# The low halves of split weights at the other end of SBUF, and a feed-forward block in four rounds

## The chip, the cores and the metric

One program runs on one core of a Trainium2 chip. The metric is the device time of one execution in microseconds (us). The kernel before was timed three times: 2065.13, 2066.44 and 2067.92 us, median 2066.44 us. One execution was profiled.

## The reference

One layer of a streaming encoder for 384 frames: 256 frames of a new stream and 16 frames each of eight running streams. All is float32.

```
h = rmsnorm(x) ; p = h @ w_in                      (2048 x 9224)
A = swish(layernorm(causal_dwconv31(GLU(p)))) @ conv_pw_out
B = fox_attention(q, k, v, logf) @ w_att_out       (past keys and values from a cache)
x = x + (sigmoid(gate_a) * A + sigmoid(gate_b) * B) @ w_out
up = rmsnorm(x) @ w_up                             (2048 x 11264; half g, half u)
x = x + (silu(causal_dwconv3(g)) * u) @ w_down     (5632 x 2048)
```

It returns the two groups' outputs, the new keys, values, forget logits, and the conv states.

## The kernel before, in words

**Split matmuls.** Each float32 operand is split into a high half `hi` (rounded to the type float32r) and a low half `lo`, the rest. One product takes three TensorE matmuls into one PSUM accumulator: high by high, high by low, low by high (lines 241 to 243 in a "B" job, where the activations are the stationary operand and the weights stream as the moving one; lines 236 to 238 in an "A" job, the other way round). `gemm` (line 219) runs a list of jobs: a B job makes a 384 x 512 piece of the output in three accumulators (one for each 128 frames), in steps of k, 128 rows of the weight each: 3 accumulators x 3 matmuls for a k.

**Weights.** They come in units of two k: SyncE's queue loads `raw` (128 x 2 x 512, line 137), ScalarE rounds it to `hi` (line 145), VectorE subtracts and gets `lo` (line 146). `raw`, `hi` and `lo` have three buffers each, and `ahead(3)` keeps three units split ahead of TensorE. The list `plan` fixes the units' order.

**Order.** TensorE's instructions stand in the order in which the code is written (`manual_schedule`). The other engines' orders are made by a scheduler with priorities: splits and evacuations of PSUM are pulled forward (`SPLIT_AHEAD`, `EVAC_AHEAD`). Each engine then works strictly through its own list.

**Feed-forward block.** Up-projection group g (of 11) is two B jobs of 16 k: the gate half and the u half of 512 columns. ScalarE evacuates each job into `tok` (line 936). VectorE turns it round with 16 block transposes (line 943), then for g the three-tap conv (964, 966), for u the product with the gate (987) and the low half of the activation (990). The result `act{g}` is a tile of the pool `acts`. In the 11th k after a g job a small transpose on TensorE (973) brings the new conv state out. `down_jobs` multiplies the `act` tiles of some groups by `w_down`: four B jobs, one for each 512 output columns, with four k for each group; VectorE adds every accumulator to the residual `y` (line 1006). `FFN_PLAN` says which groups are gathered into a down round: groups 0 to 3 after up group 4, groups 4 to 7 after up group 8, groups 8 to 10 at the end.

**PSUM.** Five accumulators of 128 x 512 (`acc`) go round in turn; a B job takes three. So the third accumulator of a job is the first one of the job before, which must have been evacuated.

**SBUF.** Pools are stacked from both ends of a partition. From the bottom: `hi` (2 to 14 KB), the pool `acts` with five slots G0 to G4 of 12 KB (14 to 76 KB; first `hT`, the normed input, then `mix`, then `act`), then `xg` (76 to 125 KB, the input of the up-projection) or, earlier, the attention's tiles. From the top: constants, `lo` (212 to 224 KB), `raw` (200 to 212 KB), then the attention output, the conv pool, or, later, `y` and the feed-forward pool. `ut`, the conv branch's 12 KB tile, uses slot G4.

Of the kernel before, what the change touches and what calls it, by code (L numbers as in the profile page):

```python
# [8 lines left out]
F32 = mybir.dt.float32  # L9
F32R = mybir.dt.float32r  # L10
# [5 lines left out]
P = 128  # L16
DM = 2048
NT = 384
# [22 lines left out]
def hybrid_step(  # L41
# [11 lines left out]
    def pool(name, side="left", bufs=1, space=None):  # L53
        kw = dict(name=name, bufs=bufs, reuse_waits="tile")
        if space is not None:
            kw["space"] = space
        else:
            kw["side"] = side
        cm = tc.tile_pool(**kw)
        p = cm.__enter__()  # L60
        return p, lambda: cm.__exit__(None, None, None)

    cp, close_cp = pool("consts", side="right")
    rp, close_rp = pool("raw_lo", side="right")
    wp, close_wp = pool("hi")
    gp, close_gp = pool("acts")
    acc, close_acc = pool("acc", bufs=5, space=PSUM)
    misc, close_misc = pool("misc", bufs=3, space=PSUM)
# [70 lines left out]
        return raw, o  # L139

    def split_tiles():
        return [p.tile([P, 2, 512], F32R, tag=tag, bufs=3, name=tag) for p, tag in ((wp, "hi"), (rp, "lo"))]

    def split_rows(hi, lo, raw, o, k):
        nc.scalar.copy(hi[:, k, :o], raw[:, k, :o])  # L145
# [2 lines left out]
    def split(raw, o):  # L148
        hi, lo = split_tiles()
        split_rows(hi, lo, raw, o, slice(0, 2))  # L150
        return hi, lo
# [3 lines left out]
    def planned(w, k0, cols, nk, *more):  # L155
        for k in range(k0, k0 + nk, 2):
            for cl in (cols,) + more:
                plan.append([w[0, k * P:(k + 2) * P, c:c + n].rearrange("(k p) n -> p k n", p=P) for c, n in cl])
# [8 lines left out]
    GA_COLS = [[(O_GA + 512 * g, 512)] for g in range(4)]  # L167
    GB_COLS = [[(O_GB + 512 * g, 512)] for g in range(4)]
    N_COLS = [[(512 * g, 512)] for g in range(4)]
    FFN_PLAN = [("up", g) for g in range(5)] + [("down", (0, 1, 2, 3))]  # L170
    FFN_PLAN += [("up", g) for g in range(5, 9)] + [("down", (4, 5, 6, 7))]
    FFN_PLAN += [("up", g) for g in range(9, 11)] + [("down", (8, 9, 10))]

    planned(w_in, 0, V_COLS[0], 16, V_COLS[1])
# [2 lines left out]
    for w, nk in ((w_att_out, 8), (conv_pw_out, 8), (w_out, 16)):  # L177
        for cols in N_COLS:
            planned(w, 0, cols, nk)
    for what, g in FFN_PLAN:  # L180
        if what == "up":
# [36 lines left out]
    def gemm(jobs, sides=()):  # L218
        for js in jobs:
            js = js if isinstance(js, tuple) else (js,)  # L220
            for j in js:
                nb = 4 if j["kind"] == "A" else NTT
                j["ps"] = [(misc_tile if j is not js[0] and i == 2 else acc_tile)() for i in range(nb)]
            for j, k in [(j, k + i) for k in range(0, js[0]["nk"], 2) for j in js for i in range(2)]:
                nb, n, nk, ps = len(j["ps"]), j["n"], j["nk"], j["ps"]
                kk = k % 2
                if kk == 0:
                    ahead(3)
                    hi, lo = ready.pop(0)
                ah, al = j["act"](k)  # L230
                st, sp = k == 0, k == nk - 1
                for m in range(nb):
                    s = slice(m * P, (m + 1) * P)
                    if j["kind"] == "A":
                        o = ps[m][:, :NT]
                        mm(o, hi[:, kk, s], ah, start=st, stop=False)  # L236
                        mm(o, hi[:, kk, s], al, start=False, stop=False)  # L237
                        mm(o, lo[:, kk, s], ah, start=False, stop=sp)  # L238
                    else:
                        o = ps[m][:, :n]  # L240
                        mm(o, ah[:, s], hi[:, kk, :n], start=st, stop=False)  # L241
                        mm(o, ah[:, s], lo[:, kk, :n], start=False, stop=False)  # L242
                        mm(o, al[:, s], hi[:, kk, :n], start=False, stop=sp)  # L243
                if sp:
                    with tc.high_priority(offset=EVAC_AHEAD):
                        for m in range(nb):
                            j["evac"](m, ps[m])
                    if "done" in j:
                        j["done"]()
                tick(sides)  # L250
# [5 lines left out]
    def job(kind, nk, act, evac, n=512, done=None):  # L256
        d = dict(kind=kind, nk=nk, act=act, evac=evac, n=n)
        if done is not None:
            d["done"] = done
        return d  # L260
# [20 lines left out]
    with tc.manual_schedule(engines={ENG.SP, ENG.Activation, ENG.DVE}):  # L281
        nc.vector.memset(junk[:, 0:1], 0.0)
        nc.scalar.dma_start(gm_row[:], norm_mix_g[0].rearrange("(c p) -> c p", p=P))
        nc.scalar.activation(junk[:, 1:2], junk[:, 0:1], AF.Identity)
        load_x(0, 1)
        first = stream_tile()
        fetch_row(first, plan[0], 0)
        load_x(1, 1)
        fetch_row(first, plan.pop(0), 1)
        second = fetch(plan.pop(0))  # L290
        load_x(2, 2)
        warm = misc_tile()

        def warm_up(n):
            for _ in range(n):
                mm(warm[:, :P], ident[:], ident[:], start=True, stop=True)

        warm_up(WARM)
        pv = misc_tile()
        tr(pv[:, :16], gm_row[:], ident[:16, :16])  # L300
        nc.vector.tensor_copy(gm[:], pv[:, :16])
        hi, lo = split_tiles()
        split_rows(hi, lo, first, V_COLS[0][0][1], slice(0, 1))
        x_chunk(0)
        warm_up(FILL)
        split_rows(hi, lo, first, V_COLS[0][0][1], slice(1, 2))
        x_chunk(1)
        ready.append((hi, lo))
        ready.append(split(*second))
# [17 lines left out]
    p_cv, close_cv = pool("conv", side="right")  # L327
# [324 lines left out]
            yield  # L652


    ut = gp.tile([P, 8, NT], F32, tag="G4", name="ut")

    sgb = [None, None]

# [88 lines left out]
    for h in range(H):  # L747
        hi, lo = aHL[h // 4][:, 0, h % 4, :], aHL[h // 4][:, 1, h % 4, :]
# [180 lines left out]
    acts = {}  # L929

    def tok_rows():
        return p_f.tile([P, NTT, 512], F32, tag="tok", bufs=1, name="tok")

    def up_evac(rows):
        def ev(t, ps):
            nc.scalar.activation(rows[:, t, :], ps[:], AF.Identity, scale=rs2[:, t:t + 1])
        return ev
# [44 lines left out]
    def up_u_done(g, rows, sg):  # L982
        def done():
            uT = p_f.tile([P, 4, NT], F32, tag="uT", bufs=1, name="uT")
            blocks(rows, lambda a, js: uT[js].rearrange("p m (t a i) -> p m t a i", t=NTT, a=4)[:, :, :, a])
            for m in range(4):
                tt(uT[:, m], uT[:, m], sg[m][:], op=ALU.mult)
                hi, lo = acts[g][:, 0, m, :], acts[g][:, 1, m, :]
                nc.scalar.copy(hi, uT[:, m])
                tt(lo, uT[:, m], f(hi), op=ALU.subtract)  # L990
        return done

    def up_jobs(g):
        sg = [p_f.tile([P, NT], F32, tag="sg", bufs=6, name="sg") for _ in range(4)]
        acts[g] = gp.tile([P, 2, 4, NT], F32R, tag=f"G{g % 5}", name=f"act{g}")
        gr, ur = tok_rows(), tok_rows()
        return [job("B", 16, xa, up_evac(gr), done=up_g_done(g, gr, sg)),
                job("B", 16, xa, up_evac(ur), done=up_u_done(g, ur, sg))]

    def down_jobs(gs, last):  # L1000
        tiles = [acts[g] for g in gs]

        def evac(n):
            def ev(t, ps):
                ys = y[:, t, n * 512:(n + 1) * 512]
                tt(ys, ps[:], ys, op=ALU.add)
                if last:
                    dst = [y_prompt[0, 0:P], y_prompt[0, P:2 * P], y_sample.rearrange("b t d -> (b t) d")][t]
                    nc.sync.dma_start(dst[:, n * 512:(n + 1) * 512], ys)
            return ev  # L1010

        return [job("B", 4 * len(gs), grouped(tiles), evac(n)) for n in range(4)]

    for what, g in FFN_PLAN:
        gemm(up_jobs(g) if what == "up" else down_jobs(g, g[-1] == 10))
# [45 lines left out]
```

## Time and profile before

| | |
|---|---|
| median of three runs | 2066.44 us |
| profiled execution, its own time | 2065.19 us |
| its span in the profile | 2063.4 us |
| TensorE (PE) busy | 2051.4 us, 9606 matmuls |
| VectorE (DVE) busy | 1189.5 us |
| ScalarE (ACT) busy | 755.7 us |
| DMA | 276.00 MB, mean 134 GB/s |
| granted TensorE clock | 0.999 of full |

A row of a group reads: line, engine, operation, output <- inputs, shape, count, then busy time in us and mean ns of one, then the engine's idle time just before these instructions and what ended it. Matmuls overlap in a pipeline, and their ends are modelled: one of 512 columns is shown with about 0.39 us, yet the next begins about 0.23 us after it. The steady pace is thus read from starts or from counts in a window, not from durations. PEld is the load of the stationary operand. Idle time in front of TensorE is the only idle time that costs something here.

### The profile page before, as it was taken

The numbers are of one execution on the slowest core, as the hardware profiler recorded it, in microseconds if no ns is written. First come the engines' busy times: TensorE is split into PE (matmuls) and PEld (weight loads), VectorE is DVE, ScalarE is ACT, GpSimd is POOL, SyncE is SP. The second block draws the span as 40 slices with busy tenths as digits, with TensorE's granted clock in tenths as the row PEclk, the third lists the DMA queues.
The fourth block names the chain that finished last, engine by engine and source line by source line (L and its number), as shares of the span: only waits on it lengthen the run. The fifth ranks groups of instructions, "written<-read, shape, count | busy, mean of one in ns | idle before, by whom it ended". The sixth has DMA issues, their size and how long they took to land.

```text
span 2063.4 us, 24707 instructions
## 1 busy us (share of the span) xinstructions
PE 2051.4 (99%) x9606; PEld 1700.8 (82%) x9606; DVE 1189.5 (58%) x1722; ACT 755.7 (37%) x1099; POOL 97.3 (5%) x214
## 2 busy tenths in 40 slices
PE   9999999999999999999999999999999999999999
PEld 8878999988888888887888888888888888888887
DVE  4434477788762645344676776533676764337662
ACT  5434455533332523333333333322333332223321
POOL 1000011100000000000000001000100100001000
PEclk9999999999999999999999999999999999999999
DMA  6555455344444353333444444344444433344443
GB/s 180 158 165 162 138 160 163 114 140 128 133 128 123 123 184 121 125 124 116 123 123 132 125 123 132 124 132 124 125 122 133 127 127 126 130 125 124 133 147 108
DMA packets 175742, 276.00 MB, mean 134 GB/s; under 512 B 11998, under 2 KB 63217, under 8 KB 175617
## 3 DMA queue, kind: packets, MB, share of 16 engines
q1 hardware_dynamic: 175305, 273.84, 43.8%
q8 instruction: 75, 1.23, 0.2%
q0 software_dynamic: 288, 0.57, 0.2%
q14 instruction: 42, 0.34, 0.1%
q10 hardware_dynamic: 32, 0.01, 0.0%
HBM read 266.98 MB, written 7.86 MB: 133 GB/s over the span
## 4 chain that ended last, share of the span: by engine, by line
PE 97%; DVE 1%; ACT 1%; DMA 0%; issue 0%; SPq 0%; ACTq 0%
PE acc L243 29%; PE acc L241 29%; PE acc L242 29%; PE acc L236 2%; PE acc L238 2%; PE acc L237 2%; DVE lo L146 0%; DMA raw<-in_w_in_dram 0%; ACT hi L145 0%; DVE uT L943 0%; PE misc L559 0%; PE misc L836 0%; PE misc L883 0%; PE misc L625 0%; PE misc L592 0%
## 5 line engine op out<-in xcount | busy, mean ns | idle before, releaser
L146 DVE TENSOR_TENSOR lo<-raw,hi 128x1024 fp32r<-128x1024 f32 (+2 forms) x481 | 580.4, 1207 | 775.1 <-ACT hi L145 768.6
L145 ACT CAST hi<-raw 128x1024 fp32r<-128x1024 f32 (+2 forms) x481 | 496.3, 1032 | 1116.9 <-PE acc L243 989.8
L241 PE MATMUL acc<-hi,xg 128*128 128x512 f32 x1056 | 418.3, 396 | 0.0
L243 PE MATMUL acc<-hi,xg 128*128 128x512 f32 x1056 | 416.0, 394 | 0.0
L242 PE MATMUL acc<-lo,xg 128*128 128x512 f32 x1056 | 414.8, 393 | 0.0
L241 PE MATMUL acc<-hi,hT 128*128 128x512 f32 (+1 forms) x704 | 271.3, 385 | 2.9 <-ACT vt L413 1.7
L243 PE MATMUL acc<-hi,hT 128*128 128x512 f32 (+1 forms) x704 | 269.3, 383 | 1.8 <-DVE hT L277 1.8
L242 PE MATMUL acc<-lo,hT 128*128 128x512 f32 (+1 forms) x704 | 268.2, 381 | 0.0
L243 PEld LDWEIGHTS acc<-hi,xg 128*128 128x128 f32 x1056 | 198.3, 188 | 47.0
L241 PEld LDWEIGHTS acc<-hi,xg 128*128 128x128 f32 x1056 | 198.2, 188 | 46.5
L242 PEld LDWEIGHTS acc<-lo,xg 128*128 128x128 f32 x1056 | 198.5, 188 | 45.4
L243 PE MATMUL acc<-hi,act 128*128 128x512 f32 x528 | 208.5, 395 | 0.2 <-DVE act L990 0.2
L241 PE MATMUL acc<-hi,act 128*128 128x512 f32 x528 | 207.8, 394 | 0.0
L242 PE MATMUL acc<-lo,act 128*128 128x512 f32 x528 | 207.0, 392 | 0.0
L243 PEld LDWEIGHTS acc<-hi,hT 128*128 128x128 f32 x704 | 132.9, 189 | 29.4 <-DVE hT L277 3.8
L241 PEld LDWEIGHTS acc<-hi,hT 128*128 128x128 f32 x704 | 133.1, 189 | 28.5 <-ACT vt L413 2.3
L711 DVE SCALAR_TENSOR_TENSOR ut<-ext,cw,ut 128x384 f32<-128x384 f32 x240 | 151.8, 632 | 6.1
L242 PEld LDWEIGHTS acc<-lo,hT 128*128 128x128 f32 x704 | 133.2, 189 | 24.8
L243 PEld LDWEIGHTS acc<-hi,act 128*128 128x128 f32 x528 | 99.1, 188 | 23.5 <-DVE act L990 0.6
L242 PEld LDWEIGHTS acc<-lo,act 128*128 128x128 f32 x528 | 99.2, 188 | 23.4
L241 PEld LDWEIGHTS acc<-hi,act 128*128 128x128 f32 x528 | 99.1, 188 | 22.3
L943 DVE STREAM_TRANSPOSE uT<-tok 32x384 f32<-32x384 f32 x176 | 100.2, 570 | 2.6
(290 smaller groups left out, 2076.4 us busy)
## 6 DMA issues: line engine op xcount, KB each, us to landing
raw<-in_w_up_dram SPq DMA_DIRECT2D x176, 512.0 KB, 3.6
raw<-in_w_in_dram SPq DMA_DIRECT2D x96, 512.0 KB, 3.6
raw<-in_w_down_dram SPq DMA_DIRECT2D x88, 512.0 KB, 3.6
raw<-in_w_in_dram SPq DMA_DIRECT2D x64, 256.0 KB, 3.0
raw<-in_w_out_dram SPq DMA_DIRECT2D x32, 512.0 KB, 3.6
raw<-in_w_att_out_dram SPq DMA_DIRECT2D x16, 512.0 KB, 3.7
raw<-in_conv_pw_out_dram SPq DMA_DIRECT2D x16, 512.0 KB, 3.5
raw<-in_w_in_dram SPq DMA_DIRECT2D x23, 344.0 KB, 3.1
```

Of the source, the lines that this page charges most:

```text
L145: nc.scalar.copy(hi[:, k, :o], raw[:, k, :o])
L146: tt(lo[:, k, :o], raw[:, k, :o], f(hi[:, k, :o]), op=ALU.subtract)
L236: mm(o, hi[:, kk, s], ah, start=st, stop=False)
L237: mm(o, hi[:, kk, s], al, start=False, stop=False)
L238: mm(o, lo[:, kk, s], ah, start=False, stop=sp)
L241: mm(o, ah[:, s], hi[:, kk, :n], start=st, stop=False)
L242: mm(o, ah[:, s], lo[:, kk, :n], start=False, stop=False)
L243: mm(o, al[:, s], hi[:, kk, :n], start=False, stop=sp)
L711: stt(o, v, wc, o, op0=ALU.mult, op1=ALU.add)
L943: nc.vector.transpose(put(a, slice(32 * b, 32 * b + 32)), src[32 * a:32 * a + 32, b])
```

## The change

`lo` leaves the top of SBUF and lies behind `hi` at the bottom (14 to 27 KB). The pool `acts` has four slots, G0 to G3, in place of five, and begins 12 KB higher (27 to 76 KB), so that `xg` stays where it was. `ut` moves into the conv pool at the upper side. `raw`, the attention output, `y` and the feed-forward pool move up by 12 KB into the room that `lo` left. With four slots, the down rounds take groups 0 to 2 (after up group 3), 3 to 5 (after 6), 6 and 7 (after 8) and 8 to 10 (after 10): four rounds in place of three. What is computed stays the same; a residual add more is made for each of the 12 pieces of `y`. Line numbers after `FFN_PLAN` are higher by one in the changed kernel.

```diff
-    rp, close_rp = pool("raw_lo", side="right")
-    wp, close_wp = pool("hi")
+    rp, close_rp = pool("raw", side="right")
+    wp, close_wp = pool("hi_lo")
...
     def split_tiles():
-        return [p.tile([P, 2, 512], F32R, tag=tag, bufs=3, name=tag) for p, tag in ((wp, "hi"), (rp, "lo"))]
+        return [wp.tile([P, 2, 512], F32R, tag=tag, bufs=3, name=tag) for tag in ("hi", "lo")]
...
-    FFN_PLAN = [("up", g) for g in range(5)] + [("down", (0, 1, 2, 3))]
-    FFN_PLAN += [("up", g) for g in range(5, 9)] + [("down", (4, 5, 6, 7))]
+    FFN_PLAN = [("up", g) for g in range(4)] + [("down", (0, 1, 2))]
+    FFN_PLAN += [("up", g) for g in range(4, 7)] + [("down", (3, 4, 5))]
+    FFN_PLAN += [("up", g) for g in range(7, 9)] + [("down", (6, 7))]
     FFN_PLAN += [("up", g) for g in range(9, 11)] + [("down", (8, 9, 10))]
...
-    ut = gp.tile([P, 8, NT], F32, tag="G4", name="ut")
+    ut = p_cv.tile([P, 8, NT], F32, name="ut")
...
-        acts[g] = gp.tile([P, 2, 4, NT], F32R, tag=f"G{g % 5}", name=f"act{g}")
+        acts[g] = gp.tile([P, 2, 4, NT], F32R, tag=f"G{g % 4}", name=f"act{g}")
```

How the instructions move, at two places.

VectorE where an up group ends and a down round of three groups begins (groups 8 to 10; this round has the same rows in both kernels). Rows of the kernel before; `y<-acc,y` are the residual adds of a down job, `lo` the weight splits:

```order
L943 STREAM_TRANSPOSE uT<-tok 32x12x32 x3
L987 TENSOR_TENSOR uT<-uT,sg 128x384 x3
L146 TENSOR_TENSOR lo<-raw,hi 128x1024
L990 TENSOR_TENSOR act_14264<-uT,act_14264 128x384 x3
L987 TENSOR_TENSOR uT<-uT,sg 128x384
L146 TENSOR_TENSOR lo<-raw,hi 128x1024
L990 TENSOR_TENSOR act_14264<-uT,act_14264 128x384
L146 TENSOR_TENSOR lo<-raw,hi 128x1024
L1006 TENSOR_TENSOR y<-acc,y 128x512 x3
L146 TENSOR_TENSOR lo<-raw,hi 128x1024 x6
```

The same engine in the changed kernel, where up group 8 ends and the new round of two groups (6 and 7) begins:

```order
L944 STREAM_TRANSPOSE uT<-tok 32x12x32 x3
L988 TENSOR_TENSOR uT<-uT,sg 128x384 x3
L146 TENSOR_TENSOR lo<-raw,hi 128x1024
L991 TENSOR_TENSOR act_12906<-uT,act_12906 128x384 x3
L988 TENSOR_TENSOR uT<-uT,sg 128x384
L1007 TENSOR_TENSOR y<-acc,y 128x512 x2
L146 TENSOR_TENSOR lo<-raw,hi 128x1024
L991 TENSOR_TENSOR act_12906<-uT,act_12906 128x384
L1007 TENSOR_TENSOR y<-acc,y 128x512
L146 TENSOR_TENSOR lo<-raw,hi 128x1024 x3
L1007 TENSOR_TENSOR y<-acc,y 128x512 x3
```

The first job of this round has 8 k in place of 12 or 16, and its adds stand inside the up group's remaining work, behind the 16 transposes, rather than behind the end of it.

TensorE of the changed kernel, with waits, where the second job of that round begins (its first row is the first one that reads `act_11332`, the tile of group 6, again):

```order
L244 MATMUL acc<-hi,act_12419 128x512
L242 MATMUL acc<-hi,act_11332 128x512 [waits Activation_49]
L243 MATMUL acc<-lo,act_11332 128x512 [waits DVE_49]
L244 MATMUL acc<-hi,act_11332 128x512
L242 MATMUL acc<-hi,act_11332 128x512
L243 MATMUL acc<-lo,act_11332 128x512
L244 MATMUL acc<-hi,act_11332 128x512
L242 MATMUL acc<-hi,act_11332 128x512 [waits DVE_49]
```

The last row is the third accumulator's first matmul: it waits for VectorE's first add of the job before. The same wait stands at each second, third and fourth job of every down round, in both kernels.

On SyncE's queue the four loads of `y` stand one weight load later each; nothing else changes there but the weights' order.

## The prediction

> **What bounds the kernel now.** I read the page's totals and chain first, then the groups of TensorE rows, then TensorE's waits.
>
> ```profile
> span 2063.4 us, 24707 instructions
> PE 2051.4 (99%) x9606; PEld 1700.8 (82%) x9606; DVE 1189.5 (58%) x1722; ACT 755.7 (37%) x1099; POOL 97.3 (5%) x214
> ...
> PE 97%; DVE 1%; ACT 1%; DMA 0%; issue 0%; SPq 0%; ACTq 0%
> ...
> PE acc L243 <- DVE hT L277: 1.8, 7, 0.4
> PE acc L241 <- ACT vt L413: 1.7, 2, 1.3
> ...
> PE acc L243 <- DVE act L990: 0.2, 1, 0.2
> ```
>
> TensorE is the bound everywhere: 97% of the chain that ended last is its own, and the longest waits listed for it inside the matmul stages are 1 to 2 us in all. The change takes no matmul away and adds none. It can gain or lose time in only two ways: the pace at which matmuls follow each other, and new waits of TensorE. The first is a matter of 7632 matmuls of 512 columns, so one nanosecond each is 7.6 us. These rows have the number of them by operand (1056 for each of three lines with `xg`, and so on):
>
> ```profile
> L241 PE MATMUL acc<-hi,xg 128*128 128x512 f32 x1056 | 418.3, 396 | 0.0
> L243 PE MATMUL acc<-hi,xg 128*128 128x512 f32 x1056 | 416.0, 394 | 0.0
> L242 PE MATMUL acc<-lo,xg 128*128 128x512 f32 x1056 | 414.8, 393 | 0.0
> L241 PE MATMUL acc<-hi,hT 128*128 128x512 f32 x576 | 227.9, 396 | 0.0
> L243 PE MATMUL acc<-hi,hT 128*128 128x512 f32 x576 | 227.0, 394 | 0.0
> L242 PE MATMUL acc<-lo,hT 128*128 128x512 f32 x576 | 226.2, 393 | 0.0
> L243 PE MATMUL acc<-hi,act 128*128 128x512 f32 x528 | 208.5, 395 | 0.2 <-DVE act L990 0.2
> L241 PE MATMUL acc<-hi,act 128*128 128x512 f32 x528 | 207.8, 394 | 0.0
> L242 PE MATMUL acc<-lo,act 128*128 128x512 f32 x528 | 207.0, 392 | 0.0
> ...
> L236 PEld LDWEIGHTS acc<-hT,hi 128*128 128x128 f32 x256 | 48.1, 188 | 1.7 <-issue 1.4
> ...
> L238 PEld LDWEIGHTS acc<-hT,lo 128*128 128x128 f32 x256 | 48.1, 188 | 0.0
> ```
>
> (`mix`, `aHL` and `zt` add 192 + 96 + 96 for each line: 3 x (1056 + 576 + 528 + 384) = 7632.)
>
> **Part one, the place of the operands.** In the kernel before, L242 streams `lo` from the top of SBUF (212 to 224 KB) and L241 and L243 stream `hi` from the bottom (2 to 14 KB). The rows show no price for the far place: L242 is the shortest of the three in each stage, 392 to 393 ns against 394 to 396. As stationary operands the two places cost the same too: 188 ns for `hi` (L236) and 188 for `lo` (L238). The activations' place shows nothing either: `act` and `hT` lie between 14 and 76 KB, `xg` between 76 and 125, and the same line differs by 2 ns at most. So I cost the move of `lo`, and that of the four slots by 12 KB, at nothing. The trace has no run with `lo` near, so both ends stay open. On the side of gain: if TensorE paid for each turn from near to far and back, L241's and L243's excess over L242 would be the price. By the rows that is 3.5 + 1.7 + 0.8 us for L241 and 1.2 + 0.8 + 1.5 for L243, 9.5 us in all, a part of which is other work between jobs. On the side of loss stands a pace that the trace does show:
>
> ```profile
> 1080.00:1140.00 60.00, 60.00 (x259) 1.00 0.45 132
> 1147.00:1207.00 60.00, 60.00 (x261) 1.00 0.43 131
> 1214.00:1274.00 60.00, 60.00 (x259) 1.00 0.45 131
> 1295.00:1355.00 60.00, 60.00 (x261) 1.00 0.39 129
> ...
> 1614.00:1674.00 60.00, 60.00 (x259) 1.00 0.45 130
> 1700.00:1760.00 60.00, 60.00 (x262) 1.00 0.40 131
> 1990.00:2050.00 60.00, 60.00 (x262) 1.00 0.40 133
> ```
>
> These are windows of 60 us, with TensorE always busy and the clock at 1.00, and the matmuls in each in brackets. There are two paces: 259 and 261 or 262 in 60 us, 231.7 and 229.9 ns a matmul with the first two counts, so the slow one costs 1.8 ns each. Neither the operands nor their places differ between the first two windows: both are up-projection, same buffers. The pace changes close to the small transposes of the next row, 11 of them, and holds until the next one.
>
> ```profile
> L973 PE MATMUL misc<-ident,lc 128*72 128x128 f32 x11 | 3.0, 271 | 0.0
> ```
>
> So the pace is a matter of phase, and which stretch gets which can be dealt anew by a change of order.
>
> The Trainium skill ("TensorE: Matmul & The Clock Gate", section "Back-to-back issue gap") gives N/2.4 + 2.5 ns between warm matmuls, 215.8 ns for 512 columns; the windows here show 14 ns more. If all of that came from where operands lie, an estimate by that page would be 108 us to gain over 7632 matmuls; the equal rows of near and far operands speak against it, and the sum does without it.
>
> **Part two, four rounds.** The weights' bytes, the matmuls and the up jobs stay. 12 adds more of `y` come, of 0.691 us each by the row below, 8.3 us on a VectorE that is busy for 1189.5 us of 2063.4: covered where VectorE has slack. If that cover is gone, TensorE waits for a free accumulator. So the place to look at is the start of each down round, where VectorE still works off the u job. In the kernel before, the last round (groups 8 to 10) shows it:
>
> ```profile
> L1006 DVE TENSOR_TENSOR y<-acc,y 128x512 f32<-128x512 f32 x36 | 24.8, 691 | 14.0 <-PE acc L243 13.9
> ...
> 1958.47 0.39 PE L243 MATMUL acc<-hi,xg 128*128 128x512 f32 x1
> 1958.70 0.40 PE L241 MATMUL acc<-hi,act 128*128 128x512 f32 x1
> ...
> 1961.13 4.05 DVE L943 STREAM_TRANSPOSE uT<-tok 32x384 f32<-32x384 f32 x7
> ...
> 1974.43 1.22 DVE L146 TENSOR_TENSOR lo<-raw,hi 128x1024 fp32r<-128x1024 f32 x1
> 1975.57 1.49 DVE L990 TENSOR_TENSOR act<-uT,act 128x384 fp32r<-128x384 f32 x3
> 1976.97 0.55 DVE L987 TENSOR_TENSOR uT<-uT,sg 128x384 f32<-128x384 f32 x1
> 1977.44 1.22 DVE L146 TENSOR_TENSOR lo<-raw,hi 128x1024 fp32r<-128x1024 f32 x1
> ...
> 1982.95 2.08 DVE L1006 TENSOR_TENSOR y<-acc,y 128x512 f32<-128x512 f32 x3 [0.42 <-PE acc L243]
> ```
>
> TensorE's round begins at U = 1958.70. VectorE works through its remainder without a pause until the last product is done at 1977.44, where its next row begins, U + 18.7. A first job of 12 k ends 12 x 9 x 0.231 = 24.9 us after U, so the add at 1982.95 waits for TensorE (0.42 us idle), not the other way round. Rounds of 16 and of 12 k are safe by 6 us or more.
>
> The new round of groups 6 and 7 has jobs of 8 k: 8 x 9 x 0.231 = 16.6 us. Its second job gets to its third accumulator 6 matmuls later, at U + 18.0, and there waits for the first add of the first job. VectorE's list has that add right behind the products, so it begins at U + 18.7 at the earliest and ends 0.69 us later, U + 19.4; with about 0.1 us of handing on, TensorE stands for **1.5 us**. Bounds: nothing if VectorE is 1.5 us ahead of that execution, and 2.7 if a weight split of 1.22 us stood before the add. Behind the waiting matmul stands all of TensorE's list, so it is a loss in full. The splits behind the adds come 1.4 us later, but these are three units (3 x 4.2 us) ahead of TensorE, and the third and fourth job find VectorE idle. The tiles `act6` and `act7` are ready: group 8 comes between or just after.
>
> Round one: groups 0 to 2 now follow up group 3 rather than 4. The stretch after group 3's transpose is the slow window at 1214 in the table, and the down jobs have no transpose that would end it. Round one's 4 x 12 x 9 = 432 matmuls then run at the slow pace: 432 x 1.8 ns = **0.8 us**. In the old order the down rounds followed fast stretches (1295, 1700, 1990).
>
> **Part three, the moves at the upper side.** `y` lies 12 KB higher, again over the attention output and the conv pool, and so waits for the same layer norm. In the trace the first load issues at 720.01:
>
> ```profile
> 720.01 0.37 SPq L866 DMA_DIRECT2D y<-in_x_prompt_dram  x1
> ...
> 721.92 0.37 SPq L137 DMA_DIRECT2D raw<-in_w_att_out_dram  x1
> ...
> 726.06 0.37 SPq L137 DMA_DIRECT2D raw<-in_conv_pw_out_dram  x1
> 726.48 0.47 SPq L866 DMA_DIRECT2D y<-in_x_prompt_dram  x1
> ```
>
> `y` is first used by the adds of `w_out`'s first job, a full stage later (line 874). A load of `y` costs the queue 0.4 to 0.5 us, and between two weight loads it has 726.06 - 721.92 = 4.1 us. With the four pairs one place later the queue still has more than 2 us to spare in each gap, and a weight load that came 2 us late would be covered by the three units ahead. **Nothing.** If the cover were gone, the queue's whole delay of 1 to 2 us would reach TensorE once. `ut` writes and reads as before, at another place; VectorE's rows on it are off TensorE's path. `act4` to `act10` find their slots free, since each slot's last reader is a down round that is over before the next up group with that slot begins.
>
> **Sum.** The profiled execution took 2065.19 us; 2065.19 + 1.5 + 0.8 = 2067.5. That execution is 1.25 us below the median of the three runs (2066.44), so the median to expect is **2068.7 us**, 0.11% above before. About 0.2%, 4.1 us, is what a measurement of this kernel can tell from no change, so this is a forecast of no change.
>
> **Rivals.**
>
> *The near place is faster.* For it: by the groups above, L241 and L243 take 1 to 3 ns longer than L242, and each three matmuls turn from near to far and back. Against it: a place that costs something should show in L242 itself, which is the shortest, and in the loads, which are equal. If the turns were the whole excess, 9.5 us go: 2068.7 - 9.5 = 2059.2. The clock-gate page's estimate would lie far below that; I give it one chance in a hundred within this rival's.
>
> *The slow pace spreads.* It ends on the other side. For it: the pace changes without a change of operand or place, so whatever shifts the phase (other addresses, the 1.5 us stop, a down round after another transpose) deals it anew, and the down rounds, in which no transpose ends a slow stretch, are the longest ones. Against it: three of the seven windows shown are slow already, so a new deal may fall either way. Four in seven of 7632 matmuls are fast now, 4361; if all turned slow, 4361 x 1.8 ns = 7.9 us: 2068.7 + 7.9 = 2076.6. It decides from about 1040 matmuls more at the slow pace (1.9 us, which with the forecast's 2.3 is over 0.2%), that is 3.6 up groups of 288.
>
> *The new round does not stop TensorE, and round one runs fast.* VectorE would have to be 1.5 us earlier than in the trace. For it: the scheduler pulled the add ahead of a split. Against it: VectorE had no pause between 1961 and 1979, so there is nothing to win. Then 2066.4.
>
> **How the numbers follow.** The forecast (no effect of place, a stop of 1.5 us, paces much as dealt) gets 0.50, with a range of its own of 2065.5 to 2071: the stop's bounds of 0 and 2.7 us, and 1 to 2 us of pace. The near place 0.22, the slow pace 0.20, no stop 0.08. For 8 times in 10 the range reaches to both other cases' full price with a little of the scatter of the runs before, 2058 to 2078. Faster by over 0.2% holds nearly all of the near place: 0.22. Slower holds nearly all of the slow pace and the upper edge of the forecast: 0.25. The rest, 0.53, is no change.
>
> **What would show it.** Right: a row in TensorE's waits for an add of `y` (L1007), once, about 1.5 us, some 18 us after the beginning of the two-group round; none like it in the other three rounds; the down jobs of the first round at 259 matmuls in 60 us; L241, L242 and L243 at the means that they have now. Wrong: windows with more than 262 matmuls in 60 us in any stage (the place matters), nearly all windows at 259 (the slow pace), or a wait of TensorE for `hi`, `lo` or a weight load around 720 us or at a round's beginning, for which no term stands here.

## The result, and the profile after

The changed kernel takes 2032.49 us against 2066.45 us of the kernel before on the same chip, a ratio of 0.983 (95% interval 0.981 to 0.985). The forecast was 2068.7 us and no change: it was wrong by 36 us, and the time lies below the range. The profiled execution of this first run took about twice the time (4122.5 us, for a reason that these runs do not show), so the rows of "after" are those of a second run of the same kernel (2032.69 us, ratio 0.984, 0.982 to 0.985; its profiled execution 2031.45 us).

From the page after: totals, the shares of the chain that ended last, and groups of TensorE's rows.

```profile
span 2029.6 us, 24719 instructions
...
PE 2014.9 (99%) x9606; PEld 1698.9 (84%) x9606; DVE 1198.4 (59%) x1734; ACT 755.2 (37%) x1099; POOL 99.4 (5%) x214
...
PE 96%; DVE 2%; ACT 1%; DMA 0%; issue 0%; SPq 0%; ACTq 0%
...
L242 PE MATMUL acc<-hi,xg 128*128 128x512 f32 x1056 | 412.9, 391 | 0.0
L244 PE MATMUL acc<-hi,xg 128*128 128x512 f32 x1056 | 411.2, 389 | 0.0
L243 PE MATMUL acc<-lo,xg 128*128 128x512 f32 x1056 | 411.1, 389 | 0.0
...
L242 PEld LDWEIGHTS acc<-hi,xg 128*128 128x128 f32 x1056 | 198.3, 188 | 42.2
```

TensorE is still the bound, with the same 9606 matmuls, and is busy for 36.5 us less (2051.4 before). All three lines became shorter, those that stream `hi` (396 to 391, 394 to 389) as much as the one that streams `lo` (393 to 389), and the weight load stays at 188 ns. So the pace rose everywhere. Five of the prediction's windows of 60 us, after:

```profile
1080.00:1140.00 60.00, 60.00 (x267) 1.00 0.43 126
1147.00:1207.00 60.00, 60.00 (x267) 1.00 0.44 132
1214.00:1274.00 60.00, 60.00 (x267) 1.00 0.40 132
1295.00:1355.00 60.00, 60.00 (x267) 1.00 0.42 123
1614.00:1674.00 60.00, 60.00 (x267) 1.00 0.44 131
```

267 matmuls stand where 259 to 261 stood (a count takes in two that only reach into the window). The two paces of before are gone; there is one, and it is faster than either. The pace is cleaner to read from starts. The timeline of TensorE in a down round, first of the kernel before, then after:

```profile
1300.15 0.39 PE L241 MATMUL acc<-hi,act 128*128 128x512 f32 x1
...
1300.84 0.40 PE L241 MATMUL acc<-hi,act 128*128 128x512 f32 x1
...
1301.54 0.39 PE L241 MATMUL acc<-hi,act 128*128 128x512 f32 x1
```

```profile
1300.06 0.39 PE L242 MATMUL acc<-hi,act 128*128 128x512 f32 x1
...
1300.74 0.39 PE L242 MATMUL acc<-hi,act 128*128 128x512 f32 x1
...
1301.42 0.39 PE L242 MATMUL acc<-hi,act 128*128 128x512 f32 x1
```

Each row begins the next three matmuls (high by high, high by low, low by high). Six of them take 1.39 us before and 1.36 us after: about 695 and 680 ns for three. "The triple" below is this time, 680 ns where TensorE is fast. Before, it is 693 or 700 ns by stretch, and 695 on the mean of all starts in the trace. 2544 triples x 15 ns = 38 us; the spans differ by 2063.4 - 2029.6 = 33.8 us, which with the one new wait of 1.6 us is 35.4, so the pace makes nearly all of it. That wait is where the prediction put it; rows of all engines in the new two-group round:

```profile
1728.49 0.39 PE L242 MATMUL acc<-hi,act 128*128 128x512 f32 x1
...
1745.94 0.39 PE L244 MATMUL acc<-hi,act 128*128 128x512 f32 x1
1746.75 0.55 DVE L988 TENSOR_TENSOR uT<-uT,sg 128x384 f32<-128x384 f32 x1
1747.22 1.28 DVE L1007 TENSOR_TENSOR y<-acc,y 128x512 f32<-128x512 f32 x2
...
1747.96 0.50 PE L242 MATMUL acc<-hi,act 128*128 128x512 f32 x1 [1.64 <-DVE y L1007]
```

The round begins at 1728.49, VectorE is through its products 18.7 us later (at 1747.22, where the first add begins), and TensorE stands for 1.64 us until the first add is done.

### The profile page after: what moved, and what is told of

It reads as the page before. It is cut to its first block, busy times and chain, and to the rows that moved or that the text cites. A ratio compares the mean times of both kernels' runs of the same rounds, so it can differ in the third digit from the quotient of the medians.

```text
span 4120.7 us, 24719 instructions
## 1 busy us (share of the span) xinstructions
PE 4113.7 (100%) x9606; PEld 2731.0 (66%) x9606; DVE 1207.5 (29%) x1734; ACT 757.9 (18%) x1099; POOL 75.5 (2%) x214
## 4 chain that ended last, share of the span: by engine, by line
PE 100%; issue 0%; POOL 0%; DVE 0%; ACT 0%; POOLq 0%
PE acc L244 30%; PE acc L242 30%; PE acc L243 30%; PE acc L238 2%; PE acc L237 2%; PE acc L239 2%; PE misc L560 0%; PE misc L837 0%; PE misc L274 0%; PE misc L884 0%; PE misc L593 0%; PE misc L587 0%; PE misc L626 0%; PE misc L612 0%; PE misc L573 0%; PE misc L577 0%
## 5 line engine op out<-in xcount | busy, mean ns | idle before, releaser
L242 PE MATMUL acc<-hi,xg 128*128 128x512 f32 x1056 | 714.3, 676 | 0.0
L244 PE MATMUL acc<-hi,xg 128*128 128x512 f32 x1056 | 712.6, 675 | 0.0
L243 PE MATMUL acc<-lo,xg 128*128 128x512 f32 x1056 | 712.2, 674 | 0.0
L242 PE MATMUL acc<-hi,hT 128*128 128x512 f32 (+1 forms) x704 | 459.1, 652 | 0.4 <-ACT vt L414 0.4
L243 PE MATMUL acc<-lo,hT 128*128 128x512 f32 (+1 forms) x704 | 455.5, 647 | 0.0
L244 PE MATMUL acc<-hi,hT 128*128 128x512 f32 (+1 forms) x704 | 455.1, 646 | 0.0
L242 PEld LDWEIGHTS acc<-hi,xg 128*128 128x128 f32 x1056 | 315.8, 299 | 178.5 <-issue 163.6
L244 PEld LDWEIGHTS acc<-hi,xg 128*128 128x128 f32 x1056 | 314.6, 298 | 178.0 <-issue 166.0
L243 PEld LDWEIGHTS acc<-lo,xg 128*128 128x128 f32 x1056 | 315.2, 299 | 174.8 <-issue 162.7
L243 PE MATMUL acc<-lo,act 128*128 128x512 f32 x528 | 356.3, 675 | 0.0
L242 PE MATMUL acc<-hi,act 128*128 128x512 f32 x528 | 356.2, 675 | 0.0
L244 PE MATMUL acc<-hi,act 128*128 128x512 f32 x528 | 356.1, 674 | 0.0
L242 PEld LDWEIGHTS acc<-hi,hT 128*128 128x128 f32 x704 | 210.3, 299 | 101.6 <-issue 87.0
L244 PEld LDWEIGHTS acc<-hi,hT 128*128 128x128 f32 x704 | 209.8, 298 | 99.3 <-issue 90.3
L242 PEld LDWEIGHTS acc<-hi,act 128*128 128x128 f32 x528 | 157.3, 298 | 89.2 <-issue 82.6
L237 PE MATMUL acc<-hT,hi 128*128 128x384 f32 x256 | 148.0, 578 | 0.0
```

## The experiments

Times are medians, and each ratio is to runs of the kernel before on the same chip. Since an address turned out to decide, the table gives for each placing where a tile group starts (thousands of bytes from the bottom of a partition) and, behind the slash, the remainder of its start address divided by 256, worked out from the addresses in the built programs. "acts" are the slots of `hT`, `mix` and `act`.

| run | `hi` | `lo` | acts | `xg` | us | ratio (95%) |
|---|---|---|---|---|---|---|
| before | 2 / 128 | 212 / 0 | 14 / 128 | 76 / 128 | 2066.4 | 1 |
| after | 2 / 128 | 14 / 128 | 27 / 128 | 76 / 128 | 2032.7 | 0.984 (0.982 to 0.985) |
| e1 | 2 / 128 | 212 / 0 | 14 / 128 | 76 / 128 | 2067.9 | 1.001 (1.000 to 1.002) |
| e2 | 2 / 128 | 14 / 128 | 27 / 128 | 88 / 128 | 2030.3 | 0.982 (0.981 to 0.984) |
| e3 | 200 / 0 | 212 / 0 | 2 / 128 | 64 / 128 | 2072.8 | 1.003 (1.002 to 1.004) |
| e4 | 212 / 0 | 2 / 128 | 14 / 128 | 76 / 128 | 2045.1 | 0.989 (0.988 to 0.991) |
| e5 | 2 / 128 | 76 / 128 | 14 / 128 | 88 / 128 | 2030.8 | 0.982 (0.981 to 0.984) |
| e6 | 2 / 128 | 14 / 128 | 151 / 0 | 27 / 128 | 2052.2 | 0.993 (0.991 to 0.994) |
| e7 | 205 / 224 | 217 / 224 | 143 / 224 | 94 / 224 | 2031.5 | 0.983 (0.981 to 0.984) |
| e8 | 2 / 128 | 212 / 128 | 14 / 128 | 76 / 128 | 2029.1 | 0.982 (0.980 to 0.983) |
| e9 | 2 / 128 | 76 / 0 | 14 / 128 | 88 / 128 | 2068.4 | 1.001 (1.000 to 1.002) |
| e11 | 200 / 128 | 212 / 128 | 2 / 128 | 64 / 128 | 2030.3 | 0.982 (0.981 to 0.984) |

**The same kernel again (e0).**

> The changed kernel again, for a profile at the full clock. All theories: 2029 to 2033 us. If the gain lies in the pace of the matmuls, 60 us windows in every stage hold 264 to 267 matmuls of 512 columns where they held 259 to 262 (34 us over some 9000 matmuls is about 4 ns each), and the one new wait of the two-group round (about 1.5 us, for an add of y) stands beside it. If the gain lies elsewhere (fewer waits), the windows stay at 259 to 262.

It gave 2032.69 us and the rows shown above.

**One part alone: the rounds (e1), the place (e2).** e1 is the kernel before with `FFN_PLAN` of the change, and `act` slots as before. e2 is the kernel before with one line changed:

```diff
-    ... for p, tag in ((wp, "hi"), (rp, "lo"))]
+    ... for p, tag in ((wp, "hi"), (wp, "lo"))]
```

> The kernel before with the four down rounds alone; five slots, and hi and lo where they were. Theory 'place' (the gain is lo's new place): 2066 to 2069 us, as the prediction had it for the rounds (a wait of 1.5 us and a little of the slow pace). Theory 'order' (the new order deals the pace anew): 2030 to 2040 us.

> The kernel before with lo moved behind hi at the bottom and nothing else; five slots, three rounds; the act slots begin at 27 KB as in the changed kernel, xg 12 KB higher (88 to 137 KB). Theory 'place': 2028 to 2034 us, 1 to 2 us under the changed kernel since the wait of the two-group round is absent; if it matters that xg's last tile lies above 128 KB, some us more. Theory 'order': 2064 to 2068 us.

The rounds alone: 2067.9 us, not to be told from no change. The place alone: 2030.3 us; its median is 2.4 us under that of the whole change, with intervals that overlap. The new wait stands among TensorE's waits in e1. Behind it the rows of L242 in e1's first and second down round (after the colon the least, median and greatest ns of one, then the first and last start in us):

```profile
PE acc L242 <- DVE y L1007: 1.3, 1, 1.3
```

```profile
L242 PE MATMUL acc<-hi,act x144: 397/397/398, 1224.4 to 1324.5; 128*128 128x512 f32 x144
...
L242 PE MATMUL acc<-hi,act x144: 391/394/396, 1525.7 to 1624.8; 128*128 128x512 f32 x144
```

144 triples lie between the starts, 143 steps: 100.1 us in the first round, 700 ns each, and 99.1 us in the second, 693 ns. The rounds alone deal the two paces of before anew and leave both there. The move of `lo` raises the pace.

**Which place? (e3, e4, e5).** e3 puts `hi` too at the top beside `lo`, e4 exchanges the two, e5 gives `lo` a pool of its own behind the activation slots.

```diff
e3  ((rp, "hi"), (rp, "lo"))
e4  ((rp, "hi"), (wp, "lo"))
e5  ((wp, "hi"), (lp_, "lo"))     # lp_: a pool opened after "acts"
```

> The kernel before with hi beside lo at the top (200 to 224 KB), the act slots at 2 to 64 KB; three rounds. Theory 'near' (TensorE pays when the streamed operand turns between far places): about 2032 us, as in the changed kernel. Theory 'bottom' (each streamed operand pays by its own address; lo at the top costs 34 us, and hi is streamed twice as often): 2066 + 2 x 34 = 2134 us. Theory 'order': 2066 us.

> The kernel before with hi and lo exchanged: hi at 212 to 224 KB, lo at 2 to 14. Two streams of three come from the top instead of one. Theory 'low': between the kernel before (2066) and both at the top (2073). Theory 'near' (turns between far places): as before, 2066, since the number of turns is the same.

> The kernel before with lo behind the act slots: lo at 76 to 88 KB, hi at 2 to 14. A step of 62 KB between them in place of 198. Theory 'low' with an edge somewhere above 88 KB: 2030 us. Theory 'low' or 'near' with a price that grows with the address or the distance: 2066 - 36 x (1 - 62/198), about 2041 us.

Both at the top is the slowest of all, 2072.8 us; the exchange lies between, 2045.1; `lo` at 76 KB, 62 KB away from `hi`, is as fast as beside it, 2030.8. The first two times are none of those that the theories gave (2032, 2134 or 2066 for e3; 2066 to 2073 for e4). The window 1147 to 1207 of e3, then of e4:

```profile
1147.00:1207.00 60.00, 60.00 (x260) 1.00 0.44 131
```

```profile
1147.00:1207.00 60.00, 60.00 (x265) 1.00 0.42 123
```

By starts, a triple takes 697 ns in e3 and 687 in e4. So neither a turn between near and far nor the distance of `hi` and `lo` decides. What remained was "the top is slow".

**Is it the top? (e6, e7).** e6 is e2 with the activation slots at the upper side; e7 is e2 with the sides of all pools exchanged, so that all operands of the matmuls lie high and `raw` at the bottom.

```diff
e6  gp, close_gp = pool("acts", side="right")
e7  kw["side"] = dict(left="right", right="left")[side]
```

> lo_only with the act slots (hT, mix, act; stationary operand of the B jobs) moved to 150 to 212 KB; hi and lo stay at the bottom, xg at 27 to 76 KB. Theory 'low, for the stationary operand too': the stages on hT, mix and act go from 226.7 to about 231 ns (1296 of 2544 groups of three, some 17 us): 2045 to 2050 us, the xg stage stays at 226.7. Theory 'low, for the stream alone': 2030 us. Theory 'near': like the first, about 2047.

> The kernel with lo beside hi (lo_only), every SBUF pool put on the other side: hi and lo at 205 to 229 KB, act slots at 143 to 205, xg at 94 to 143, raw and the constants at the bottom. All that TensorE reads in a stage lies as near to each other as in lo_only. Theory 'near' (what counts is the distance between operands): 2028 to 2033 us and 226.7 ns a matmul. Theory 'low' (what counts is how high each operand lies): 2070 us or more, 231 to 234 ns.

Two windows of e6, the first in the up-projection (stationary operand `xg`, low), the second in a down round (stationary operand `act`, high):

```profile
1147.00:1207.00 60.00, 60.00 (x267) 1.00 0.45 132
1295.00:1355.00 60.00, 60.00 (x260) 1.00 0.38 124
```

One kernel has a fast and a slow pace, by the tile that is stationary, though the streamed operands are the same; the whole is 2052.2 us, just over the 2045 to 2050 on record. And e7, with everything high, is as fast as e2 (2031.5 us). So height isn't it, nor whether the operand is streamed or stationary. The distance between stationary and streamed operand, by which e7's time had been forecast rightly, isn't it either: in e2 `xg3` lies 111 KB above the end of `hi` and is fast, in the kernel before it ends 87 KB below `lo` and is slow. The theory of the place had fallen. Two were left. By the **remainder**: the two stacks of pools begin at addresses with different remainders, and every kernel that was slow so far (before, e1, e3, e4, e6) pairs tiles from the two stacks. By the **neighbour**: in each of these the slow operand lies in the area of `raw`, where the DMAs write.

**The remainder, mapped (e10).** e2 with unused tiles between the activation tiles, so that each has its own offset from the weights:

```diff
-    hT = [gp.tile([P, 2, 4, NT], F32R, tag=f"G{g}", name=f"hT{g}") for g in range(4)]
+    hT = []
+    for g, pad in enumerate((0, 8, 8, 16)):
+        if pad:
+            gp.tile([P, pad], F32, name=f"pad{g}")
+        hT.append(gp.tile([P, 2, 4, NT], F32R, tag=f"G{g}", name=f"hT{g}"))
+    gp.tile([P, 32], F32, name="pad4")
...
+        for g, pad in enumerate((32, 32, 96, 80)):     # ahead of xg0 to xg3
```

> This kernel is e2 (low halves moved behind the high halves, three rounds) with small unused tiles between the activation tiles, so that each activation tile has a start address of its own relative to the streamed weights: against the weights' start, modulo 4096 bytes, G0 lies at 0, G1 at 32, G2 at 64, G3 at 128, G4 at 256, xg0 at 384, xg1 at 512, xg2 at 896 and xg3 at 1216. In e2 all lie at 0. Theory 'alignment' (what costs is a stationary operand and a streamed operand whose addresses differ modulo some power of two; the top of SBUF is slow only because the tiles there stand 896 bytes off): within this one kernel the time of three 512-column matmuls, start to start, is 680 ns for G0 and 690 to 700 ns for some of the others, and which ones tells the modulus: 256 if G4 and xg1 are at 680 and G3, xg0, xg2, xg3 are not; 512 if only G0 and xg1 are. The total then lies between 2035 and 2062 us. Rival 'raw neighbour' (operands pay that lie in the upper area beside the tiles that the weight DMAs write): no tile has moved out of its area, so every tile stays at 680 ns and the total is that of e2, 2030 +- 2 us.

2057.8 us (ratio 0.995, 0.994 to 0.997): the tiles did not all stay at 680 ns. Each activation tile is used for 36 matmuls in a row, 12 triples, in a job. TensorE's timeline, the rows at which the next tile begins: first in a job of the first down round (`act0` to `act3` and the next job), then in one of the second (`act4` to `act7`), then in an up job (`xg0` to `xg3`):

```profile
1286.82 0.40 PE L241 MATMUL acc<-hi,act 128*128 128x512 f32 x1
...
1295.01 0.39 PE L241 MATMUL acc<-hi,act 128*128 128x512 f32 x1
...
1303.40 0.40 PE L241 MATMUL acc<-hi,act 128*128 128x512 f32 x1
...
1311.80 0.39 PE L241 MATMUL acc<-hi,act 128*128 128x512 f32 x1
...
1320.16 0.39 PE L241 MATMUL acc<-hi,act 128*128 128x512 f32 x1
...
1685.95 0.40 PE L241 MATMUL acc<-hi,act 128*128 128x512 f32 x1
...
1694.13 0.39 PE L241 MATMUL acc<-hi,act 128*128 128x512 f32 x1
...
1702.30 0.39 PE L241 MATMUL acc<-hi,act 128*128 128x512 f32 x1
...
1710.69 0.40 PE L241 MATMUL acc<-hi,act 128*128 128x512 f32 x1
```

```profile
1486.55 0.39 PE L241 MATMUL acc<-hi,xg 128*128 128x512 f32 x1
...
1494.95 0.40 PE L241 MATMUL acc<-hi,xg 128*128 128x512 f32 x1
...
1503.13 0.40 PE L241 MATMUL acc<-hi,xg 128*128 128x512 f32 x1
...
1511.50 0.39 PE L241 MATMUL acc<-hi,xg 128*128 128x512 f32 x1
...
1519.75 0.39 PE L241 MATMUL acc<-hi,xg 128*128 128x512 f32 x1
```

The differences, divided by 12:

| tile | offset from the weights, bytes | remainder by 256 | 36 matmuls, us | triple, ns |
|---|---|---|---|---|
| act0, act5 | 0 | 0 | 8.19, 8.17 | 682, 681 |
| act1, act6 | 32 | 32 | 8.39, 8.39 | 699, 699 |
| act2 | 64 | 64 | 8.40 | 700 |
| act3 | 128 | 128 | 8.36 | 697 |
| act4 | 256 | 0 | 8.18 | 682 |
| xg0 | 384 | 128 | 8.40 | 700 |
| xg1 | 512 | 0 | 8.18 | 682 |
| xg2 | 896 | 128 | 8.37 | 697 |
| xg3 | 1216 | 192 | 8.25 | 688 |

The fast tiles are those at 0, 256 and 512 bytes, and no other. 128 lies between two of them and is slow, so of the powers of two it is 256. A difference of 192 costs 8 ns a triple, one of 64 costs 20; 192 was tried with one tile alone.

**The cure and the counter-test (e8, e9, e11).** If the remainder is the cause, 128 unused bytes should make the kernel before fast with `lo` left where it was, and the fast e5 slow. e8 is the kernel before, e11 is e3, each with the same two lines (and one that closes the pool); e9 is e5 with a 128-byte tile ahead of `lo` and one behind it.

```diff
     cp, close_cp = pool("consts", side="right")
+    pp, close_pp = pool("pad", side="right")
+    pp.tile([P, 32], F32, name="pad")
```

> The kernel before with one unused tile of 128 bytes a partition between the constants and the low halves, and nothing else: the low halves stay at the top of SBUF, three rounds stay, the low halves' start is now 209,664 bytes above the high halves', a multiple of 256 (before: 209,792, which is 128 more than a multiple of 256). Theory 'alignment modulo 256 bytes': every triple of 512-column matmuls goes to 680 ns as in e2, and the total is 2030 us (2027 to 2034): the whole gain of the change, with the operands 200 KB apart as before. Rival 'raw neighbour' and every rival that goes by the place (the low halves pay where they lie beside the tiles that the weight DMAs write, or at the top): the place is the same to 128 bytes, so 2066 to 2068 us, triples at 688 and 698 ns.

> e5 (low halves behind the activation tiles, at 76 KB; 2030.8 us) with 128 unused bytes a partition ahead of the low halves and 128 behind them, so that the low halves alone stand 128 bytes off the other operands modulo 256, and the tiles behind them stand as before modulo 256. Theory 'alignment modulo 256 bytes': the pattern of the kernel before at the bottom of SBUF, triples at 688 to 700 ns, total 2066 us (2061 to 2070). Rivals by place: no operand is at the top or beside the tiles that the DMAs write, so 2031 us, triples at 680 ns.

> e3 (high and low halves both at the top beside the tiles that the DMAs write; 2072.8 us, the slowest placing so far) with one unused tile of 128 bytes a partition between the constants and them, so that both stand a multiple of 256 bytes above the activations. Theory 'alignment modulo 256 bytes': 2030 us (2027 to 2034), triples at 680 ns. Rival 'raw neighbour': both streamed operands still lie beside the tiles that the DMAs write, so 2073 us, triples at 690 to 706 ns.

2029.1, 2068.4 and 2030.3 us: each as the remainder says, to 2.4 us, and against the neighbour by some 37 us or more. The window 1147 to 1207 of e8, e9 and e11, one row of each (the kernel before has 261 here, the quicker of its two paces):

```profile
1147.00:1207.00 60.00, 60.00 (x266) 1.00 0.43 130
```

```profile
1147.00:1207.00 60.00, 60.00 (x262) 1.00 0.43 128
```

```profile
1147.00:1207.00 60.00, 60.00 (x267) 1.00 0.43 125
```

Two more readings fall by the addresses of the same programs. The pad shifts `raw` and the rest of the upper stack too, but `raw` has remainder 0 in the fast e2 and e5 as in the slow e9. And it is the difference that counts, not a good remainder of 128: in e7 all operands have 224, and it is fast.

e8 is the best version: the kernel before with 128 idle bytes, three rounds and `lo` at the top has the whole gain, and not the wait of the fourth round. It beats the kernel before by 1.8% (0.980 to 0.983); its median is 3.6 us under that of the changed kernel, though the intervals overlap. It differs from e2 by less than these runs tell apart.

What stays open is the mechanism below the rule. In the timeline the load of the next stationary operand (0.19 us) runs while the matmul before it streams; that both read SBUF at the same time is a likely reason for a cost that depends on the two addresses, but no run kept the load from running beside a stream. Nor does any run say why 192 is cheaper than 64, or why e4, with two of three products off, loses less (2045) than the kernel before, with one off (2066). The price isn't one of the single product either. In the kernel before, the next start comes on the mean 232.0 and 232.2 ns after the two products with `hi`, whose remainder fits, and 230.7 after the one with `lo`, whose doesn't; after the change it is 227 each. So a product off slows its neighbours as well, and the rule is shown for what it does to the stream of all three, not for a matmul by itself.

## Why the prediction was wrong, and where it was right

**Part one, the place of the operands: the step that failed.** It read "I cost the move of `lo` ... at nothing", with 9.5 us as the most that could be gained. It was worth 36 us (2066.4 to 2030.3, e2). The failure has three layers.

- *The rows compared could not show the price.* L242 being the shortest of the three lines was taken as proof that the far place is free. But one operand with the wrong remainder slowed all three lines alike (396, 394, 393 against 391, 389, 389, and by starts 232, 231 and 232 ns against 227): a price that is common to all lines has no trace in their differences. The 9.5 us were worked out from those differences, so this was no bound at all. The duration column misled too, since these rows overlap: only starts and counts show the pace.
- *Near and far was the wrong variable.* "The activations' place shows nothing either" was true, and proved nothing: `act`, `hT` and `xg` came from one stack and all had the remainder 128. Only `lo` had another, and it took part in every triple, so no stretch of the trace lacked the price.
- *The one sign there was, was left.* Before, the pace had two values with no change of operands, and the prediction saw it 14 ns over a figure of the Trainium skill ("TensorE: Matmul & The Clock Gate", section "Back-to-back issue gap"), which that section gives for an isolated matmul. By starts the paces were 231.1 and 233.3 ns, 15 and 18 ns over that figure; the prediction's 229.9 and 231.7 came from counts that take in two matmuls that only reach into the window. After, a fast triple is 680 ns, 226.7 ns a matmul: still 11 ns above it. So about a third of the gap was real gain here, and the rest is not explained by these runs.

The Trainium skill ("SBUF — State Buffer", section "SBUF: two separate sides") has TensorE wait for no one at SBUF's engine ports. Whether a wait at a port is behind the price, no run shows. But nobody should read from that sentence that TensorE's pace is free of where its operands lie: the runs have 681 and 699 ns for a triple, at offsets of 0 and 32 bytes between its two SBUF operands (act5 and act6 of e10).

**The rival "The near place is faster"** had the right sign and part, but not the cause: e8 is as fast with `lo` far as e2 with it near, and e9 is slow with it nearer than before. The prediction named windows with more than 262 matmuls as what would show that the place matters; 267 came.

**Part two, the new wait: right.** Forecast 1.5 us at U + 18.0, with VectorE's products done at U + 18.7 and the add at U + 19.4. After: products done at 1747.22, U + 18.7; TensorE goes on at 1747.96, U + 19.5; wait 1.64 us. In e1 it is 1.3 us. There is no such row for the other rounds.

**Part two, round one at the slow pace: right in e1, without object after.** e1's first round runs at 700 ns a triple, the slow pace; its profiled span is 3.0 us longer than before (2066.4 - 2063.4), where the two terms made 2.3. The term of 0.8 us was a little small: by starts the two paces are 2.2 ns a matmul apart, not the 1.8 that the counts gave, so 144 triples x 6.7 ns = 1.0 us. In the changed kernel there is no slow pace left. The cause given, a phase that the small transposes set, holds at most for the second order: two paces for the same operands were seen only where remainders differ (before, e1, e9), while e2, e5, e7, e8 and e11 have one.

**Part three, the moves at the upper side, at nothing: no run speaks against it.** No wait for `y`'s loads or for `ut` stands among TensorE's waits after. The medians of e2 and of the whole change, 2.4 us apart, leave little room for it: 1.6 us of them are the wait.

**"The slow pace spreads"** came in e1 in a small way only. Three of the four jobs of its last round also stand at 700 ns, which the forecast had not named: 108 triples x 6.7 ns = 0.7 us, far from the 7.9 of this rival. With the 1.0 us of the first round and the wait of 1.3 they make up the 3.0 us.

## What to carry to other kernels

Before a row is taken to show that something costs nothing, ask whether the trace holds any stretch without it: a cost that is in all rows can't be seen in their differences, and the bound has to come from somewhere else, here from the pace that TensorE does not reach. In float32r kernels of this shape, give stationary and streamed operands start addresses with the same remainder by 256 bytes; pools that are stacked from both ends of SBUF can break this silently, and here one tile of 128 idle bytes repaired it. Any change that moves tiles can have this as a hidden second effect, so test it with a placing that keeps the remainders.

## What was not expected of the hardware

The pace of these float32r matmuls of 512 columns depends on the offset between the stationary operand's address and the streamed ones': 227 ns each where it is a multiple of 256 bytes for all three products, 229 to 233 ns at the other offsets tried (32, 64, 128 and 192 bytes beyond one), with the granted clock at 0.998 to 0.999 throughout and weight loads of 188 ns in both (e10). It makes no difference which of them lies high or low in SBUF (e7, e11), or how far they are apart (e5: 62 KB between `hi` and `lo`; e8: 200 KB).
